# Splitting each weight unit in one piece of 1024 columns instead of two halves of 512

## The chip, the cores and the metric

The kernel runs on one NeuronCore of a Trainium2 chip. The metric is the device time of one execution in microseconds (us). A core has a matmul engine (TensorE, PE in the profile, with PEld for its weight loads), VectorE (DVE), ScalarE (ACT), GpSimd (POOL) and SyncE (SP). Each engine works through its own list of instructions strictly in order; semaphores make an engine wait for another, and DMAs are issued from the lists of SP (queue q1) and ACT (queue q10).

## The reference

A two-layer bidirectional encoder over 512 tokens of width 1024, in float32:

```python
for i in range(DEPTH):                                  # 2 layers
    h = rms_norm(x, norm_mix_g[i])
    q, k, v, u_f, u_s, gates = split(h @ w_in[i])       # 7168 columns
    o = diff_attention(rotary(q), rotary(k), v, lam)    # 8 heads
    y_a = (rms_norm(o, attn_subln_g[i]) * (1 - lam_init)) @ w_attn_br[i]
    y_b = fourier_mix(u_f) @ w_fourier_br[i]
    z = gelu(s5_mix(u_s, ...)) @ w_glu[i] + b_glu[i]    # state-space layer
    y_c = z[..., :D] * sigmoid(z[..., D:])
    g = sigmoid(gates)
    x = x + (g_a * y_a + g_b * y_b + g_c * y_c) @ w_out[i]
    up = rms_norm(x, norm_ffn_g[i]) @ w_up[i]           # 2 x 2816 columns
    x = x + (gelu(conv3(up[..., :D_FF])) * up[..., D_FF:]) @ w_down[i]
    x = x + sigmoid(rms_norm(x, norm_ple_g[i]) @ w_ple_gate[i]) * (p[i] @ w_ple[i])
return rms_norm(x, final_norm_g)
```

## The kernel before

Every large product is done with operands split into a high part that TensorE multiplies fast (float32r) and a low remainder, and three matmuls stand for one: high by high, low by high, high by low (`mm`, L101). Activations are kept transposed: tile `hh`/`hl` number k holds 128 of the 1024 features for all 512 tokens.

Weights come in units of 128 x 1024 float32 (512 KB). A unit is one output tile of 128 columns with all eight k-tiles of 128, so the product of one unit is 24 matmuls of 512 columns into one PSUM bank. `unit` (L85) fetches a unit with one DMA on SP's list into `wr` (two buffers), and then splits it: ACT copies `wr` to the high part `wh`, DVE subtracts that from `wr` to give the low part `wl`. It does so in two halves of 512 columns, each in buffers of its own, six of `wh` and six of `wl`, which all units share. A half holds four k-tiles; its buffer comes free when the last matmul that reads those four k-tiles is done. `unit_wide` (L478) does the same for the V projection with POOL in place of DVE, and `row_unit` (L1056) for the last stage, most of it in 14 buffers of its own pool.

The order of each engine's list is not written out: a scheduler plans it at build time from priorities, data and free buffers, with buffers handed out in the order in which they come free in its plan. It is static on the chip.

A layer runs thus: norm, state-space parameters and Fourier mixing (s5_params, `fourier`); attention by heads (`head`, L520) with the state-space tables (`s5_tables`, L373, POOL) in the background; then the branch products. For what follows one place matters: the turn from attention to the branch products (L821 to L841). There the last head's output `oh`/`ol` number 7 is made; `s5_toeplitz` (L440) and `s5_gather_u` (L608, `U<-usd`, eight DMAs of 16 x 32 x 64 elements) issue many DMAs from ACT's list; and TensorE does the eight products with `w_attn` (L840). A `w_attn` unit multiplies `oh` 0 to 7: its first half needs heads 0 to 3 alone, its second half heads 4 to 7. TensorE starts three of these products early, in three banks `w` of PSUM, and finishes them when the last head is there. After them come eight state-space chunks (`s5_chunk`, L616) mixed with gate and Fourier products, the GLU (L877), `w_out`, the MLP (L919 and L942) and the gated embedding (L970, `ple_last` L988). In the GLU two units at a time (`w2`, then `w1`) serve two output tiles each.

Of the kernel before, what the change touches and what calls it, by code (L numbers as in the profile page):

```python
# [9 lines left out]
F32 = mybir.dt.float32  # L10
F32R = mybir.dt.float32r
I32 = mybir.dt.int32
AF = mybir.ActivationFunctionType
ALU = mybir.AluOpType
# [4 lines left out]
P = 128  # L19
# [31 lines left out]
class Kernel:  # L51
# [33 lines left out]
    def unit(self, src, cols=1024):  # L85
        nc = self.nc
        raw = self.t(self.wp, "wr", (P, 1024), bufs=2)
        nc.sync.dma_start(raw[:, :cols], src)
        out = []
        for c in range(0, cols, 512):  # L90
            n = min(512, cols - c)
            hi = self.t(self.wp, "wh", (P, 512), F32R, bufs=6)
            lo = self.t(self.wp, "wl", (P, 512), F32R, bufs=6)
            nc.scalar.activation(hi[:, :n], raw[:, c:c + n], AF.Copy)  # L94
            nc.vector.tensor_tensor(out=lo[:, :n], in0=raw[:, c:c + n],  # L95
                                    in1=hi[:, :n].bitcast(F32), op=ALU.subtract)
            for i in range(n // P):
                out.append((hi[:, i * P:(i + 1) * P], lo[:, i * P:(i + 1) * P]))
        return out

    def mm(self, ps, w, xh, xl, start=True, stop=True):  # L101
        nc = self.nc
# [171 lines left out]
    def s5_params(self, i, keep, pool, R):  # L274
# [18 lines left out]
        def unit(c, sn):  # L293
# [5 lines left out]
            V.tensor_tensor(out=sn, in0=sn, in1=t, op=ALU.mult)  # L299

        unit(c, sn)
        Wr = self.t(keep, "Wr", (P, 8, n))
        Wi = self.t(keep, "Wi", (P, 8, n))
# [32 lines left out]
        for k in range(3):  # L336
# [3 lines left out]
            V.tensor_tensor(out=c8, in0=t, in1=u, op=ALU.subtract)  # L340
            src = (c8, s8)
        unit(c8, s8)

        ph = []
# [133 lines left out]
    def unit_wide(self, src):  # L478
        nc = self.nc
        raw = self.t(self.wp, "wr", (P, 1024), bufs=2)  # L480
        nc.sync.dma_start(raw, src)
        out = []
        for c in range(0, 1024, 512):
            hi = self.t(self.wp, "wh", (P, 512), F32R, bufs=6)
            lo = self.t(self.wp, "wl", (P, 512), F32R, bufs=6)
            nc.scalar.activation(hi, raw[:, c:c + 512], AF.Copy)
            nc.gpsimd.tensor_tensor(out=lo, in0=raw[:, c:c + 512], in1=hi.bitcast(F32), op=ALU.subtract)
            out += [(hi, lo, 0), (hi, lo, 256)]
        return out

    def qk_proj(self, i, ar, ap, m, tag, hh, hl, cosr, sinr, z=None):
        nc = self.nc
# [563 lines left out]
    def row_unit(self, pool, src, own):  # L1056

        nc = self.nc
        raw = self.t(self.wp, "wr", (P, 1024), bufs=2)
        nc.sync.dma_start(raw, src)  # L1060
        out = []
        for c in range(0, 1024, 512):
            hi = self.t(pool, "lwh", dt=F32R, bufs=14) if own else self.t(self.wp, "wh", dt=F32R, bufs=6)
            lo = self.t(pool, "lwl", dt=F32R, bufs=14) if own else self.t(self.wp, "wl", dt=F32R, bufs=6)
            self.split(raw[:, c:c + 512], hi, lo)
            out.append((hi, lo))
        return out

    def v_pair(self, i, ap, hp, hh, hl, rc):
        nc = self.nc  # L1070
# [149 lines left out]
```

## Time and profile before

| what | value |
|---|---|
| time before, median of 3 runs | 2235.33 us (2235.26 to 2237.52) |
| the profiled execution's own time | 2237.99 us |
| its span in the profile | 2236.2 us |
| TensorE busy | 2121.7 us, 95% |
| VectorE busy | 1534.3 us, 69% |
| ScalarE busy | 1023.5 us, 46% |
| GpSimd busy | 760.2 us, 34% |

The span is what the profile sees from the first to the last instruction; all positions below count from its start. Layer 0 runs to about 1136 us and layer 1 from there on: attention from 110 to 417 and from 1200 to 1517, the turn to the branch products from 417 to 446 and from 1517 to 1546. An instruction's duration is in its row; a number in brackets behind a row is the time that the engine stood idle before it, and what ended that. Matmuls overlap, so the distance from start to start is what one costs on TensorE, not its duration.

### The profile page before, as it was taken

Reading aid. Unit: us, or ns where it says so; the run is one execution under the profiler, and the core shown is the slowest. Engines: PE = TensorE matmul, PEld = TensorE weight load, DVE = VectorE, ACT = ScalarE, POOL = GpSimd, SP = SyncE. Lnnn points to the kernel's source line nnn. Section 1 sums busy time; section 2 is a strip of 40 time slices with the busy share of each in tenths; the row PEclk is TensorE's granted clock in tenths of the full one; section 3 lists DMA queues with packets and bytes.
Section 4 is the critical chain, followed back from the end, with each engine's and each line's share of the span. In section 5 each row is a group of like instructions: output and inputs, shape, how many; then the busy total and the mean of one; then the engine's idle time right before and its main releaser. Section 6 shows DMA issues by size and latency. Waiting matters only on the chain.

```text
span 2236.2 us, 29074 instructions
## 1 busy us (share of the span) xinstructions
PE 2121.7 (95%) x10432; PEld 1772.2 (79%) x10432; DVE 1534.3 (69%) x2664; ACT 1023.5 (46%) x1900; POOL 760.2 (34%) x748
## 2 busy tenths in 40 slices
PE   7888989899999999999998898898999999999998
PEld 5777778688888888888887787687888888888886
DVE  7988997566666766633689899984666667665344
ACT  4256665244434444433442766552445444444333
POOL 4497876223101322200025967841330012221000
PEclk9999999999999999999998999999999999999999
DMA  5232232665323333233432322236743323333341
GB/s 186 79 110 78 86 101 97 190 222 197 116 94 95 97 102 95 92 95 97 149 118 80 105 87 90 97 123 186 259 150 107 97 90 101 97 95 96 95 130 57
DMA packets 117232, 259.20 MB, mean 116 GB/s; under 512 B 43456, under 2 KB 49856, under 8 KB 115040
## 3 DMA queue, kind: packets, MB, share of 16 engines
q1 hardware_dynamic: 87040, 218.48, 31.3%
q10 hardware_dynamic: 30048, 38.87, 5.2%
q8 instruction: 82, 1.34, 0.3%
q14 instruction: 62, 0.51, 0.1%
HBM read 216.87 MB, written 40.37 MB: 115 GB/s over the span
## 4 chain that ended last, share of the span: by engine, by line
PE 69%; DVE 13%; POOL 6%; DMA 5%; ACT 3%; issue 2%; ACTq 0%; SPq 0%; DVEq 0%; POOLq 0%
PE w L106 55%; PE s L106 5%; DVE wl L95 2%; DMA tab<-tb 1%; PE s L639 1%; DVE mx L541 1%; DMA U<-usd 1%; PE w L1079 1%; POOL ra L501 1%; POOL tb L417 1%; DVE tb L402 1%; DVE pr L553 1%; PE w L1026 1%; PE w L1028 1%; PE w L1027 1%
## 5 line engine op out<-in xcount | busy, mean ns | idle before, releaser
L95 DVE TENSOR_TENSOR wl<-wr,wh 128x512 fp32r<-128x512 f32 x596 | 465.5, 785 | 303.5 <-ACT wh L94 295.6
L94 ACT ACTIVATE wh<-wr 128x512 fp32r<-128x512 f32 x596 | 368.5, 624 | 631.4 <-PE w L106 424.7
L106 PE MATMUL w<-hh,wh 128*128 128x512 f32 x1536 | 607.8, 396 | 20.1 <-DVE rs L499 9.0
L106 PE MATMUL w<-hl,wh 128*128 128x512 f32 x1536 | 604.8, 394 | 2.3 <-DVE hl L82 2.2
L106 PE MATMUL w<-hh,wl 128*128 128x512 f32 x1536 | 604.6, 394 | 1.6 <-DVE wl L95 1.6
L106 PEld LDWEIGHTS w<-hh,wh 128*128 128x128 f32 x1536 | 291.6, 190 | 82.5 <-DVE rs L499 10.6
L106 PEld LDWEIGHTS w<-hl,wh 128*128 128x128 f32 x1536 | 291.2, 190 | 63.5 <-DVE hl L82 5.0
L106 PEld LDWEIGHTS w<-hh,wl 128*128 128x128 f32 x1536 | 290.9, 189 | 62.0 <-DVE wl L95 2.2
L180 POOL TENSOR_TENSOR sq<-sq,sq 128x512 f32<-128x512 f32 x18 | 25.0, 1391 | 454.0 <-ACT sq L178 454.0
L191 POOL TENSOR_TENSOR ge<-ge,cv 128x512 f32<-128x512 f32 x44 | 57.8, 1315 | 305.3 <-DVE ge L190 305.3
L106 PE MATMUL w<-ah,wl 128*128 128x512 f32 x352 | 140.4, 399 | 0.0
L106 PE MATMUL w<-al,wh 128*128 128x512 f32 x352 | 138.7, 394 | 0.0
L106 PE MATMUL w<-ah,wh 128*128 128x512 f32 x352 | 138.0, 392 | 0.0
L546 ACT ACTIVATE pr<-s,mx 128x512 f32<-128x512 f32 x128 | 87.9, 689 | 54.5 <-DVE mx L541 49.2
L541 DVE TENSOR_REDUCE mx<-s 128x1 f32<-128x512 f32 x128 | 85.7, 678 | 8.9 <-PE s L540 8.9
L936 POOL TENSOR_TENSOR uu<-uu,cv 128x512 f32<-128x512 f32 x44 | 58.2, 1323 | 71.9 <-DVE cv L193 71.9
L106 PEld LDWEIGHTS w<-al,wh 128*128 128x128 f32 x352 | 66.1, 188 | 17.1
L539 PE MATMUL s<-ks,qs 128*128 128x512 f32 x128 | 56.9, 450 | 23.7 <-ACT pr L546 23.0
L106 PEld LDWEIGHTS w<-ah,wh 128*128 128x128 f32 x352 | 66.1, 188 | 15.8
L106 PEld LDWEIGHTS w<-ah,wl 128*128 128x128 f32 x352 | 66.1, 188 | 15.3
L106 PE MATMUL w<-oh,wh 128*128 128x512 f32 x128 | 52.6, 421 | 14.8 <-DVE m L841 6.5
L553 DVE SCALAR_TENSOR_TENSOR pr<-pr,c,pr 128x512 f32<-128x512 f32 x64 | 65.8, 1028 | 1.0
(417 smaller groups left out, 4227.3 us busy)
## 6 DMA issues: line engine op xcount, KB each, us to landing
wr<-in_w_in SPq DMA_DIRECT2D x112, 512.0 KB
wr<-in_w_up SPq DMA_DIRECT2D x88, 512.0 KB
tb<-tab SPq DMA_DIRECT2D x16, 1536.0 KB
tab<-tb ACTq DMA_DIRECT2D x64, 256.0 KB
wr<-in_w_down SPq DMA_DIRECT2D x32, 512.0 KB
tab<-vbt ACTq DMA_DIRECT2D x32, 256.0 KB
wr<-in_w_attn SPq DMA_DIRECT2D x16, 512.0 KB
wr<-in_w_glu SPq DMA_DIRECT2D x16, 512.0 KB
```

The lines of the kernel that those rows point to most:

```text
L94: nc.scalar.activation(hi[:, :n], raw[:, c:c + n], AF.Copy)
L95: nc.vector.tensor_tensor(out=lo[:, :n], in0=raw[:, c:c + n], in1=hi[:, :n].bitcast(F32), op=ALU.subtract)
L106: nc.tensor.matmul(ps, lhsT=w[i][a], rhs=b[i], start=start and i == 0 and q == 0, stop=stop and i == n - 1 and q == 2)
L180: eng.tensor_tensor(out=sq, in0=sq, in1=acc[c], op=ALU.add)
L191: nc.gpsimd.tensor_tensor(out=sq, in0=sq, in1=y, op=ALU.mult)
L402: nc.vector.tensor_tensor(out=vb, in0=vb, in1=t2, op=ALU.add)
L417: G.tensor_tensor(out=ct, in0=wsel(prm["Wr"], d, d == 1), in1=bsel(2), op=ALU.mult)
L539: nc.tensor.matmul(s, lhsT=q[:, c, qs], rhs=kk[:, c], start=True, stop=False)
L541: V.tensor_reduce(mx[:, c:c + 1], s, op=ALU.max, axis=AX.X, negate=True)
L546: nc.scalar.activation(pt, ss[c], AF.Exp, bias=mx[:, c:c + 1], accum_out=(s1, s2)[c][:, qt:qt + 1])
L553: V.scalar_tensor_tensor(out=pr[0], in0=pr[1], scalar=c2, in1=pr[0], op0=ALU.mult, op1=ALU.add)
L936: G.tensor_tensor(out=u, in0=u, in1=c, op=ALU.mult)
```

## The change

All three helpers split a unit in one instruction per engine, into buffers of 1024 columns, three of `wh` and three of `wl` (seven in the last stage's own pool): the bytes are the same. What reads the parts reads slices of the large buffer. The lists are planned anew by the scheduler.

```diff
@@ unit
-        out = []
-        for c in range(0, cols, 512):
-            n = min(512, cols - c)
-            hi = self.t(self.wp, "wh", (P, 512), F32R, bufs=6)
-            lo = self.t(self.wp, "wl", (P, 512), F32R, bufs=6)
-            nc.scalar.activation(hi[:, :n], raw[:, c:c + n], AF.Copy)
-            nc.vector.tensor_tensor(out=lo[:, :n], in0=raw[:, c:c + n],
-                                    in1=hi[:, :n].bitcast(F32), op=ALU.subtract)
-            for i in range(n // P):
-                out.append((hi[:, i * P:(i + 1) * P], lo[:, i * P:(i + 1) * P]))
-        return out
+        hi = self.t(self.wp, "wh", (P, 1024), F32R, bufs=3)
+        lo = self.t(self.wp, "wl", (P, 1024), F32R, bufs=3)
+        nc.scalar.activation(hi[:, :cols], raw[:, :cols], AF.Copy)
+        nc.vector.tensor_tensor(out=lo[:, :cols], in0=raw[:, :cols], in1=hi[:, :cols].bitcast(F32),
+                                op=ALU.subtract)
+        return [(hi[:, c:c + P], lo[:, c:c + P]) for c in range(0, cols, P)]
@@ unit_wide
-        for c in range(0, 1024, 512):
-            hi = self.t(self.wp, "wh", (P, 512), F32R, bufs=6)
-            lo = self.t(self.wp, "wl", (P, 512), F32R, bufs=6)
-            nc.scalar.activation(hi, raw[:, c:c + 512], AF.Copy)
-            nc.gpsimd.tensor_tensor(out=lo, in0=raw[:, c:c + 512], in1=hi.bitcast(F32), op=ALU.subtract)
-            out += [(hi, lo, 0), (hi, lo, 256)]
-        return out
+        hi = self.t(self.wp, "wh", (P, 1024), F32R, bufs=3)
+        lo = self.t(self.wp, "wl", (P, 1024), F32R, bufs=3)
+        nc.scalar.activation(hi, raw, AF.Copy)
+        nc.gpsimd.tensor_tensor(out=lo, in0=raw, in1=hi.bitcast(F32), op=ALU.subtract)
+        return [(hi, lo, c) for c in range(0, 1024, 256)]
@@ row_unit
-            hi = self.t(pool, "lwh", dt=F32R, bufs=14) if own else self.t(self.wp, "wh", dt=F32R, bufs=6)
-            lo = self.t(pool, "lwl", dt=F32R, bufs=14) if own else self.t(self.wp, "wl", dt=F32R, bufs=6)
-            self.split(raw[:, c:c + 512], hi, lo)
-            out.append((hi, lo))
-        return out
+        hi = self.t(pool, "lwh", (P, 1024), F32R, bufs=7) if own else self.t(self.wp, "wh", (P, 1024), F32R, bufs=3)
+        lo = self.t(pool, "lwl", (P, 1024), F32R, bufs=7) if own else self.t(self.wp, "wl", (P, 1024), F32R, bufs=3)
+        self.split(raw, hi, lo)
+        return [(hi[:, c:c + 512], lo[:, c:c + 512]) for c in (0, 512)]
```

What the new plan does to ACT's list at the turn of layer 0. Before, `wh_5018` and `wh_5022` are the two halves of the fifth `w_attn` unit, `wh_5054` and `wh_5058` those of the sixth; the fourth unit stands further up.

```order
L94 ACTIVATE wh_5018<-wr_5016 128x512
L452 DMA dtab_276<-kfb_1008 128x512
...
L81 ACTIVATE oh_4125<-og_4098,gsub_208 128x512
L78 ACTIVATE ffh_5165<-fraw_5163 128x512
L613 DMA U_4175<-usd_277 16x32x64 x8
L94 ACTIVATE wh_5022<-wr_5016 128x512
L94 ACTIVATE wh_5054<-wr_5052 128x512
L94 ACTIVATE wh_5058<-wr_5052 128x512
```

Now, in the same place, with `wh_4810` for the fourth `w_attn` unit and `wh_4842` for the fifth:

```order
L81 ACTIVATE oh_3997<-og_3970,gsub_204 128x512
L78 ACTIVATE ffh_4973<-fraw_4971 128x512
L605 DMA U_4047<-usd_273 16x32x64 x8
L91 ACTIVATE wh_4810<-wr_4808 128x1024
L91 ACTIVATE wh_4842<-wr_4840 128x1024
```

The split of the whole fourth unit and of the first half of the fifth stood ahead of the eight U DMAs, and stands behind them now. Layer 1 has the same move (`wh_14947` ahead of `U_14104` before; `wh_14091` and `wh_14123` behind `U_13328` now).

TensorE's list at that place, before: `w_4954` is the third `w_attn` product, `w_4990` the fourth (halves `wh_4982` and `wh_4986`), `w_5026` the fifth (halves `wh_5018` and `wh_5022`).

```order
L106 MATMUL w_4954<-oh_4125,wl_4951 128x512
L106 MATMUL w_4990<-oh_1538,wh_4982 128x512
L106 MATMUL w_4990<-ol_1539,wh_4982 128x512
...
L106 MATMUL w_4990<-oh_4125,wl_4987 128x512
L106 MATMUL w_5026<-oh_1538,wh_5018 128x512
...
L106 MATMUL w_5026<-oh_2638,wl_5019 128x512
L106 MATMUL w_5026<-oh_3094,wh_5022 128x512
```

And now: `w_4782` is the third product, `w_4814` the fourth, `w_4846` the fifth.

```order
L101 MATMUL w_4782<-oh_3997,wl_4779 128x512
L101 MATMUL w_4814<-oh_1490,wh_4810 128x512
L101 MATMUL w_4814<-ol_1491,wh_4810 128x512
L101 MATMUL w_4846<-oh_1490,wh_4842 128x512
L101 MATMUL w_4846<-ol_1491,wh_4842 128x512
L101 MATMUL w_4814<-oh_1490,wl_4811 128x512
```

TensorE's sequence of products is the same, but each of the two units is one pair of buffers now, and two matmuls of the fifth product have moved ahead of the fourth's first use of a low part.

## Rows read from the trace of the kernel before

**Rows 1.** The page: busy time, share and instructions of each engine.
```profile
PE 2121.7 (95%) x10432; PEld 1772.2 (79%) x10432; DVE 1534.3 (69%) x2664; ACT 1023.5 (46%) x1900; POOL 760.2 (34%) x748
```

**Rows 2.** Busy time by stretch; columns in the first line.
```profile
core 0: us, PE busy (x) PEld busy (x) DVE busy (x) ACT busy (x) POOL busy (x), PEclk, DMA share, GB/s
...
310.00:360.00 50.00, 44.56 (x216) 36.89 (x215) 45.16 (x77) 33.04 (x71) 35.51 (x33) 0.93 0.26 86
...
417.00:446.00 29.00, 21.57 (x100) 16.62 (x98) 9.56 (x22) 3.79 (x6) 1.36 (x3) 0.94 0.87 231
446.00:612.00 166.00, 165.29 (x883) 141.43 (x884) 106.25 (x143) 78.33 (x130) 42.74 (x35) 1.00 0.58 181
...
1546.00:1720.00 174.00, 174.00 (x914) 148.28 (x915) 110.20 (x150) 80.74 (x134) 42.71 (x35) 0.99 0.55 175
```

**Rows 3.** Chain of waits, MLP of layer 0: start, length, what.
```profile
719.53 353.64 PE w L106 x1543
```

**Rows 4.** Timeline of ACT, turn of layer 0: start, length, engine, line, instruction.
```profile
427.88 0.72 ACT L81 ACTIVATE oh<-og,gsub 128x512 fp32r<-128x512 f32 x1 [3.50 <-DMA dtab<-kfb]
432.97 0.63 ACT L78 ACTIVATE ffh<-fraw 128x512 fp32r<-128x512 f32 x1 [4.38 <-DMA tb<-tab]
432.99 12.99 ACTq L613 DMA_DIRECT2D U<-usd  x8
446.02 1.67 ACT L94 ACTIVATE wh<-wr 128x512 fp32r<-128x512 f32 x3 [12.42 <-DMA U<-usd]
```

**Rows 5.** Timeline of TensorE, same place (36 matmuls from the first to the third row).
```profile
435.04 0.80 PE L106 MATMUL w<-oh,wh 128*128 128x512 f32 x1 [3.94 <-DVE m L841]
...
437.33 0.63 PE L106 MATMUL w<-oh,wl 128*128 128x512 f32 x1
...
444.66 0.40 PE L106 MATMUL w<-oh,wl 128*128 128x512 f32 x1
446.71 0.50 PE L106 MATMUL w<-oh,wh 128*128 128x512 f32 x1 [1.65 <-ACT wh L94]
```

**Rows 6.** Busy time by stretch: those 36 matmuls of layer 0, and layer 1's.
```profile
434.90:446.60 11.70, 10.02 (x36) 7.75 (x36) 1.28 (x3) 0.58 (x2) 0.00 (x0) 0.87 1.20 237
1532.30:1545.90 13.60, 10.22 (x36) 7.82 (x36) 1.25 (x3) 0.63 (x2) 0.00 (x0) 0.87 1.05 225
```

**Rows 7.** Timeline of ACT, turn of layer 1.
```profile
1530.36 14.86 ACTq L613 DMA_DIRECT2D U<-usd  x8
1545.27 1.67 ACT L94 ACTIVATE wh<-wr 128x512 fp32r<-128x512 f32 x3 [14.30 <-DMA U<-usd]
```

**Rows 8.** Timeline of TensorE, turn of layer 1 (36 matmuls to the second row).
```profile
1532.41 0.50 PE L106 MATMUL w<-oh,wh 128*128 128x512 f32 x1 [2.56 <-DVE m L841]
...
1542.24 0.39 PE L106 MATMUL w<-oh,wl 128*128 128x512 f32 x1
1545.95 0.50 PE L106 MATMUL w<-oh,wh 128*128 128x512 f32 x1 [3.33 <-ACT wh L94]
```

**Rows 9.** ACT by line and shape: count, busy, mean ns, idle before.
```profile
L94 ACT ACTIVATE wh<-wr 128x512 fp32r<-128x512 f32 x580 | 361.8, 630 | 618.2 <-PE w L106 420.2 <-issue 54.6 <-PE s L106 35.9
...
L505 ACT ACTIVATE ks<-ra 128x1024 fp32r<-128x1024 f32 x16 | 16.9, 1057 | 11.4 <-POOL ra L501 8.2 <-DVE c L552 3.0
```

**Rows 10.** DVE by line and shape, whole span.
```profile
L95 DVE TENSOR_TENSOR wl<-wr,wh 128x512 fp32r<-128x512 f32 x580 | 458.8, 795 | 303.5 <-ACT wh L94 295.6 <-PE w L106 4.1
...
L95 DVE TENSOR_TENSOR wl<-wr,wh 128x256 fp32r<-128x256 f32 x16 | 6.7, 416 | 0.0
```

**Rows 11.** DVE by line and shape, 720 to 1074, then 110 to 417.
```profile
L95 DVE TENSOR_TENSOR wl<-wr,wh 128x512 fp32r<-128x512 f32 x125 | 89.0, 712 | 99.2 <-ACT wh L94 95.4 <-PE w L106 2.0
...
L95 DVE TENSOR_TENSOR wl<-wr,wh 128x512 fp32r<-128x512 f32 x49 | 49.9, 1024 | 7.1 <-ACT wh L94 7.1
```

**Rows 12.** Chain of waits by line, 110 to 417.
```profile
by line: PE w L106 12.1%; issue 6.9%; DMA tab<-tb 5.4%; POOL ra L501 4.4%; POOL rs L500 3.6%; POOL tb L417 3.5%; DVE wl L95 3.4%; DVE mx L541 3.0%; DVE pr L553 2.8%; DMA tab<-vbt 2.6%; ACT pr L546 2.4%; POOL tb L401 2.4%; POOL tb L240 2.4%;
```

**Rows 13.** Chain of waits, 417 to 447.
```profile
416.55 0.74 POOL tb L243
```

More of the change, by code (lines that the diff above doesn't have):

```diff
@@ L481, in unit_wide @@
         nc.sync.dma_start(raw, src)
-        out = []
-        for c in range(0, 1024, 512):
-            hi = self.t(self.wp, "wh", (P, 512), F32R, bufs=6)
-            lo = self.t(self.wp, "wl", (P, 512), F32R, bufs=6)
-            nc.scalar.activation(hi, raw[:, c:c + 512], AF.Copy)
-            nc.gpsimd.tensor_tensor(out=lo, in0=raw[:, c:c + 512], in1=hi.bitcast(F32), op=ALU.subtract)
-            out += [(hi, lo, 0), (hi, lo, 256)]
-        return out
+        hi = self.t(self.wp, "wh", (P, 1024), F32R, bufs=3)
[3 more added lines that the diff above has]
+        return [(hi, lo, c) for c in range(0, 1024, 256)]
     def qk_proj(self, i, ar, ap, m, tag, hh, hl, cosr, sinr, z=None):
@@ L1060, in row_unit @@
         nc.sync.dma_start(raw, src)
-        out = []
-        for c in range(0, 1024, 512):
-            hi = self.t(pool, "lwh", dt=F32R, bufs=14) if own else self.t(self.wp, "wh", dt=F32R, bufs=6)
-            lo = self.t(pool, "lwl", dt=F32R, bufs=14) if own else self.t(self.wp, "wl", dt=F32R, bufs=6)
-            self.split(raw[:, c:c + 512], hi, lo)
-            out.append((hi, lo))
-        return out
+        hi = self.t(pool, "lwh", (P, 1024), F32R, bufs=7) if own else self.t(self.wp, "wh", (P, 1024), F32R, bufs=3)
+        lo = self.t(pool, "lwl", (P, 1024), F32R, bufs=7) if own else self.t(self.wp, "wl", (P, 1024), F32R, bufs=3)
+        self.split(raw, hi, lo)
+        return [(hi[:, c:c + 512], lo[:, c:c + 512]) for c in (0, 512)]
     def v_pair(self, i, ap, hp, hh, hl, rc):
```

## The prediction

> **What bounds the kernel now.** I read the page's busy shares first, then busy time by stretch, then the chain of waits and the timelines at the places where TensorE stops. TensorE is busy 95% of the span [rows 1], and outside attention practically without a gap: 165.29 of 166 us behind the turn of layer 0, 174.00 of 174 behind that of layer 1 [rows 2]. In the MLP one piece of the chain is 1543 matmuls in 353.64 us, 0.229 us each [rows 3], so a unit of 24 matmuls keeps TensorE for 5.5 us. There, shortening a split gains nothing; what makes TensorE late before such a stretch is paid in full. In attention TensorE and VectorE share the bound (44.56 and 45.16 of 50 us in one slice [rows 2]). And at the turn from attention to the branch products, 29 us with 21.57 busy [rows 2], neither computes what the end waits for: ScalarE's list is held for 12.99 us by the eight U DMAs, and in layer 1 for 14.86 [rows 4, 7].
>
> **The shorter splits.** A DVE split takes 416 ns at 256 columns [rows 10] and 690 to 712 at 512 where nothing disturbs it (712 in the MLP [rows 11]); 256 columns more cost about 0.28 us, so 1024 take about 1.25 us, estimated from these rows, and two halves 1.4: 0.15 us saved per unit. ACT takes 630 ns for 512 and 1057 for 1024 [rows 9]: 0.20 saved. Over some 300 units that is 60 us of ACT and 45 of DVE, but nearly all of it in stretches in which TensorE is the bound. What can count is attention. There a 512 split takes 1024 ns, not 712 [rows 11]: 0.31 us of each is something that the row doesn't explain, presumably GpSimd's work beside it. If that is paid once per instruction, a merged pair saves 0.15 + 0.31 = 0.46 us; if it grows with the columns, 0.15. The middle is 0.31. The 49 splits between 110 and 417 are some 24 pairs: 7.4 us of DVE time a layer. But splits are 3.4% of that stretch's chain [rows 12], 10.4 of their own 49.9 us, a fifth; a fifth of 7.4 is 1.5 a layer, **-3 us** for both. The ends: nothing, or all of 24 x 0.46 x 2 = 22 us if every split were on the chain. Upwards: a DVE instruction of 1.25 us holds what is queued behind it (the softmax maxima, the transposed probabilities) 0.55 us longer than one of 0.7; if each of the 24 stood before such work, 13 us a layer, 26 in all. I take none of this, since the two halves stood in the same list before and only what stood between them is moved.
>
> On the lock between DVE and GpSimd the Trainium skill (SBUF — State Buffer, section "SBUF: two separate sides") says that the loser waits for the whole instruction of the other, when DVE reads two SBUF inputs. The rows' 1024 ns against 712 agree with waits of that kind, but don't tell how many there are. By the rule a pair would save the 0.46 above, and the sum would be 1 us lower.
>
> **Buffers that come free by units.** In the steady stretches two units are ready while a third buffer is refilled: 1.06 us of ACT and 1.25 of DVE, against 5.5 us for each unit in hand. Nothing is lost: TensorE's work hides it, and without that cover it would be 2.3 us a unit. In the GLU two of three buffers are held by the two units in use. The plan hands out the buffer of the unit that ends first, with its pair's last 12 matmuls (2.75 us) still to run; the low part is needed two matmuls later, at 3.2 us, and is there at 2.3 us plus what ACT and DVE have queued ahead. That is tight but fits: zero, with up to 0.9 us for each of three changes of units a layer, 5 us in all, if the queue ahead is longer. At the program's start and in the last stage a whole unit is ready 1 us later than its first half; DMAs and norms cover this: zero, or 2 us.
>
> **The turn.** Here the change costs. Three `w_attn` products wait for the last head with their units in the buffers. Before, the first halves of these units, which need heads 0 to 3 alone, had been read early; their three buffers held the whole fourth unit and the first half of the fifth, split before ACT came to the U DMAs. That is the 36 matmuls that TensorE ran from 435.04 on while ACT was held [rows 5], and 36 again from 1532.41 [rows 8]. Now no buffer is free before the last head has been multiplied. The plan puts both splits behind the U DMAs, and TensorE, whose list has these products next, must wait.
>
> Step by step for layer 0. ACT is free at 446.02 [rows 4]. It splits the fourth unit until 447.08 and the fifth until 448.1; TensorE can begin at 447.14, with the same 0.06 us as before (446.02 + 0.63 to 446.71, rows 4 and 5). It does the two matmuls of each that need a high part alone, and is done with them, and has the first low part (447.1 + 1.25 = 448.4), at about 449.0. Then 44 matmuls remain: 44 x 0.229 = 10.1, to 459.1. Before, at 446.71, 12 of the fifth product remained, to 449.5. Lost: 9.6 us. TensorE stood idle before both runs of 36, and in both its clock was the lower level for a while: granted 0.87 over the stretch [rows 6], and 9.62 us from first to last [rows 5] where 35 x 0.229 is 8.0; in layer 1 9.83 [rows 8]. Before, this 1.6 to 1.8 us lay in time that TensorE waited out anyway; now it is on the path, 0.8 of it already counted with the first four matmuls. So 9.6 + 0.6 to 1.0: about 10.3 a layer. In layer 1 ACT comes free at 1545.27 and TensorE went on at 1545.95 [rows 7, 8], the same distance. Behind each turn TensorE has no gap in which to catch up [rows 2]. **+20.5 us** for both. The ends: nothing, if the U DMAs begin early enough for attention to cover them; 24 us, if the lower clock lasts through more of the products.
>
> **Sum.** -3 + 20.5 = +17.5 on the profiled execution's 2237.99 gives 2255.5. That execution was 2.66 us above the median of the runs, so 2252.8 on the median's scale; I say **2252 us**.
>
> **Rivals.**
> *Attention slows as well.* The longer DVE instructions stand before the maxima and probabilities. For it: DVE is busy nine tenths there. Against: as many columns stood in the list before. Half of the 26 us: 2252 + 13 = 2265.
> *The lock and the fixed costs are the bound.* DVE's saving counts for its most of 22 us, not 3. For it: 1024 against 712 ns. Against: splits are a fifth of their own time on the chain. 2252 - 19 = 2233; with half of it, 2242. By the skill's rule above, as far as it alone goes, 2251; this rival needs the chain to be DVE's as well.
> *The change does nothing at the turn, the kernel is faster.* The chain at the turn begins with the last table on GpSimd, at 416.55 [rows 13], then DMAs, then U. If lighter ACT and DVE lists let the tables end earlier while attention's TensorE work still runs, the U DMAs lie under attention. It decides once they begin some 10 us earlier in each layer: then 20.5 us go, and the 3 stay, 2235.3 - 3 = 2232; the gaps of 1.65 and 3.33 us [rows 5, 8] could go too, 2227. Against: lists that are 7 us a layer shorter, a fifth of that on the chain, are not 10 us earlier.
> *Part of the way.* The U DMAs begin 3 to 5 us earlier in each layer: 2252 - 8 = 2244.
>
> **How the numbers follow.** The forecast, 2246 to 2258 as its own range: 0.60. Part of the way: 0.12. Attention slower: 0.14. DVE's saving in full, about 2233 to 2242: 0.07. No cost at the turn: 0.07. Faster or slower by 0.2% is 4.5 us, about what a measurement of this kernel tells from no change: below 2230.9 or above 2239.8. Faster gets most of the last case and a little of the one before, 0.07. Same gets the rest of the last and much of the one before, 0.07. Slower has 0.86. The range leaves out the last case and part of the neighbours below, and the tail of slower attention: 2239 to 2266.
>
> **What would show it.** In the profile after: no `w_attn` matmuls between the last head's and the end of the U DMAs; a wait of about 16 us of TensorE for the high part at each turn (before: 3.94 + 1.65 and 2.56 + 3.33 with 36 matmuls between); then the fourth product; TensorE still without gaps behind it; about 300 splits of some 1.25 us in the MLP on DVE and 1.06 on ACT. The distance from the end of the U DMAs to the end of layer grows by about 10 us in each layer, and attention (110 to 417) is a few us shorter or equal. I am wrong if the wait at the turn is under 10 us, if attention moves by more than 6 us either way in a layer, or if the GLU shows waits for low parts of more than 1 us each.

## The result: slower by about 1%

The changed kernel takes 2258.69 us (median of 4 runs, 2253.38 to 2260.49), the kernel before 2236.07 beside it (4 runs, 2235.26 to 2237.52): 1.0097 times as long, interval 1.0079 to 1.0114. The forecast was 2252, range 2239 to 2266. The profiled execution took 2260.49 us, its span is 2258.7: 22.5 more than before. What follows is read on the spans of these two profiled executions.

The page of the changed kernel, answering to [rows 1]:

```profile
PE 2123.6 (94%) x10432; PEld 1777.1 (79%) x10432; DVE 1475.2 (65%) x2356; ACT 960.5 (43%) x1576; POOL 762.5 (34%) x732
```

DVE has 59 us less to do and ACT 63 (45 and 60 were worked out ahead), and TensorE practically the same. On balance none of the 122 us came back as time.

The turn of layer 0 in the changed kernel, ACT's timeline (start, length, engine, line, instruction; the bracket is the idle time before it and what ended that), answering to [rows 4]:

```profile
423.65 0.72 ACT L81 ACTIVATE oh<-og,gsub 128x512 fp32r<-128x512 f32 x1 [2.81 <-DMA dtab<-kfb]
427.81 0.63 ACT L78 ACTIVATE ffh<-fraw 128x512 fp32r<-128x512 f32 x1 [3.45 <-DMA tb<-tab]
427.83 13.31 ACTq L605 DMA_DIRECT2D U<-usd  x8
441.19 2.00 ACT L91 ACTIVATE wh<-wr 128x1024 fp32r<-128x1024 f32 x2 [12.74 <-issue]
```

TensorE at the same place, answering to [rows 5]:

```profile
426.48 0.40 PE L101 MATMUL w<-oh,wl 128*128 128x512 f32 x1
442.30 0.80 PE L101 MATMUL w<-oh,wh 128*128 128x512 f32 x1 [15.42 <-ACT wh L91]
442.89 0.63 PE L101 MATMUL w<-ol,wh 128*128 128x512 f32 x1
443.32 0.72 PE L101 MATMUL w<-oh,wh 128*128 128x512 f32 x1
443.84 0.63 PE L101 MATMUL w<-ol,wh 128*128 128x512 f32 x1
444.26 0.63 PE L101 MATMUL w<-oh,wl 128*128 128x512 f32 x1
...
447.25 0.51 PE L101 MATMUL w<-oh,wh 128*128 128x512 f32 x1
447.60 0.39 PE L101 MATMUL w<-ol,wh 128*128 128x512 f32 x1
```

and at the turn of layer 1, answering to [rows 8]:

```profile
1542.66 0.40 PE L101 MATMUL w<-oh,wl 128*128 128x512 f32 x1
1559.11 0.79 PE L101 MATMUL w<-oh,wh 128*128 128x512 f32 x1 [16.04 <-ACT wh L91]
```

ACT's list has the eight U DMAs first and both high-part splits behind them. The third `w_attn` product ends at 426.9, and then TensorE has nothing until 442.30; before, 36 matmuls ran here. After the wait of 15.42 us the distances from start to start are 0.43 us (two of them 0.52 and 0.59) up to 447.25 and 0.23 from 447.60 on. The granted clock of these 5 us (busy time by stretch):

```profile
442.30:447.30 5.00, 5.00 (x12) 3.69 (x13) 2.94 (x3) 1.93 (x3) 0.00 (x0) 0.50 1.14 177
```

0.50, the lower level of 1.2 GHz, behind a wait in which TensorE did nothing.

Where the 22.5 us are is found by cutting the span at the end of the third `w_attn` product and the start of the MLP, in both layers. As the start of the MLP counts DVE's first read of an MLP product (`gp`) in layer 0 and TensorE's next matmul behind that read in layer 1; the differences come out the same by either. These two stretches in the kernel before (columns as in [rows 2]):

```profile
431.10:718.80 287.70, 282.12 (x1390) 236.40 (x1391) 173.73 (x256) 122.99 (x203) 46.96 (x44) 0.99 0.50 152
1529.90:1820.50 290.60, 284.77 (x1392) 237.87 (x1392) 173.80 (x257) 123.27 (x204) 46.92 (x44) 0.99 0.49 151
```

and in the changed kernel:

```profile
426.90:726.40 299.50, 283.53 (x1392) 237.26 (x1392) 166.19 (x213) 115.25 (x159) 48.31 (x44) 0.97 0.49 146
1543.10:1843.00 299.90, 283.40 (x1393) 237.03 (x1393) 165.94 (x214) 116.07 (x160) 48.84 (x44) 0.97 0.49 146
```

The same work, some 1390 matmuls, takes 11.8 us longer in layer 0 and 9.3 in layer 1, together 21.1. Of this, 10.6 and 9.1 are lost by the end of the 48th matmul behind the cut, the work of two products (449.84 before and 456.20 now; 1550.40 and 1572.71). Behind it come 1.4 us more, of which a wait of TensorE for a table (508.50, layer 0) is 0.57; the others were not traced. The rest follows from the ends of these stretches: to the first cut the changed kernel is 4.2 us earlier (431.1 to 426.9); from the MLP of layer 0 to the cut of layer 1 it takes 816.7 us, not 811.1, 5.6 more; from the MLP of layer 1 to the end 415.7 in both. -4.2 + 11.8 + 5.6 + 9.3 = 22.5.

### The profile page after: what moved, and what is told of

The parts are those of the page before. It is cut to its first block, busy times and chain, and to the rows that moved or that the text cites. A ratio compares the mean times of both kernels' runs of the same rounds, so it can differ in the third digit from the quotient of the medians.

```text
span 2258.7 us, 28154 instructions
## 1 busy us (share of the span) xinstructions
PE 2123.6 (94%) x10432; PEld 1777.1 (79%) x10432; DVE 1475.2 (65%) x2356; ACT 960.5 (43%) x1576; POOL 762.5 (34%) x732
## 4 chain that ended last, share of the span: by engine, by line
PE 71%; DVE 15%; POOL 5%; DMA 4%; ACT 2%; issue 2%; ACTq 1%; SPq 0%; DVEq 0%; POOLq 0%
PE w L101 57%; PE s L101 4%; DVE wl L92 2%; DMA tab<-tb 1%; PE s L631 1%; DVE mx L533 1%; DMA tb<-tab 1%; PE o L555 1%; DMA U<-usd 1%; DVE tb L397 1%; POOL tb L412 1%; DVE pr L545 1%; PE m L405 1%; PE w L1068 1%; DVE tb L414 1%
## 5 line engine op out<-in xcount | busy, mean ns | idle before, releaser
L92 DVE TENSOR_TENSOR wl<-wr,wh 128x1024 fp32r<-128x1024 f32 (+1 forms) x298 | 384.7, 1292 | 220.3 <-ACT wh L91 216.8
L91 ACT ACTIVATE wh<-wr 128x1024 fp32r<-128x1024 f32 (+1 forms) x298 | 311.7, 1047 | 460.1 <-PE w L101 317.0
L82 DVE SCALAR_TENSOR_TENSOR al<-uu,ah 128x512 fp32r<-128x512 f32 x44 | 32.6, 741 | 80.9 <-ACT ah L81 80.9
```

The source lines that it names most:

```text
L82: nc.vector.scalar_tensor_tensor(out=lo, in0=src, scalar=scale, in1=hi.bitcast(F32), op0=ALU.mult, op1=ALU.subtract)
L91: nc.scalar.activation(hi[:, :cols], raw[:, :cols], AF.Copy)
L92: nc.vector.tensor_tensor(out=lo[:, :cols], in0=raw[:, :cols], in1=hi[:, :cols].bitcast(F32), op=ALU.subtract)
```

## The experiments

Theory A, the prediction's: the cost is the turn, because both high parts stand behind the U DMAs that hold ACT. Theory B: the long instructions or the wide buffers cost in themselves, at the turn or elsewhere. Theory C, from the second set on: a hold of ACT costs wherever the U DMAs are issued. "Third product to MLP" below is the stretch just shown. Each ratio is against runs of the kernel before on the same chip.

**Big buffers, small instructions** (`e1_big_buffers_small_splits`): the buffers of 1024 columns stay, each filled by two instructions per engine. `unit` is shown; `unit_wide` and `row_unit` are changed alike.

```diff
-        nc.scalar.activation(hi[:, :cols], raw[:, :cols], AF.Copy)
-        nc.vector.tensor_tensor(out=lo[:, :cols], in0=raw[:, :cols], ...)
+        for c in range(0, cols, 512):
+            e = min(c + 512, cols)
+            nc.scalar.activation(hi[:, c:e], raw[:, c:e], AF.Copy)
+            nc.vector.tensor_tensor(out=lo[:, c:e], in0=raw[:, c:e], ...)
```

> Buffers of 1024 columns, three of each, as in the changed kernel, but each unit split by two instructions of 512 columns as before. Theory A (the cost is that a buffer comes free only with its whole unit, so that ACT's splits of the fourth and fifth w_attn units fall behind the U DMAs): the wait of about 15 us for the high part at each turn stays, and the time is 2250 to 2262 us. Theory B (the cost is the longer split instructions, which hold up what is queued behind them in attention): without them the time is back at 2236 to 2241, and the turn has no such wait.

2273.39 us, 1.0167 [1.0147, 1.0187], some 15 us above the changed kernel. TensorE's timeline at the turn of layer 0 in this kernel:

```profile
458.83 0.79 PE L102 MATMUL w<-oh,wh 128*128 128x512 f32 x1 [12.35 <-ACT wh L93]
```

The wait is there without any long instruction, and 13.48 us in layer 1; third product to MLP is 297.8 and 296.3, 10.1 and 5.7 more than before. So the wait comes with the buffers, and B's long instructions are refuted as its cause. But the expected time was missed on the high side: the third product ends at 446.5, 15.4 us later than before. DVE's splits between 110 and 417 don't explain it (44 instructions and 47.4 us, against 49 and 49.9 in [rows 11]); the plan has put other lists together. Why these lists are so much worse stays open.

**U DMAs from SP's list, changed kernel** (`e2_after_u_on_sp`):

```diff
-            nc.scalar.dma_start(U[j * 16:(j + 1) * 16], v[j])
+            nc.sync.dma_start(U[j * 16:(j + 1) * 16], v[j])
```

> The changed kernel with the eight U DMAs issued from SP's list instead of ACT's; ACT's order is otherwise the same. Theory A: ACT splits the fourth w_attn unit right behind the ffh copy, about 12 us earlier at each turn, and TensorE works through two or three units while U lands: 10 us gained per turn, 2236 to 2243 us. If it is DMA traffic or attention that costs (theory B), the time stays at 2253 to 2260. If SP's list is held instead and the weights come late, something between, with TensorE waiting for w_attn units from the third one on.

2250.06 us, 1.0062 [1.0045, 1.0079]; third product to MLP 295.0 and 294.2. ACT's timeline at the turn of layer 0 and TensorE's:

```profile
427.25 0.63 ACT L78 ACTIVATE ffh<-fraw 128x512 fp32r<-128x512 f32 x1 [3.08 <-DMA U<-usd]
427.79 1.99 ACT L91 ACTIVATE wh<-wr 128x1024 fp32r<-128x1024 f32 x2
```

```profile
429.74 0.47 PE L101 MATMUL w<-oh,wh 128*128 128x512 f32 x1 [3.06 <-DVE m L833]
...
431.98 0.79 PE L101 MATMUL w<-oh,wl 128*128 128x512 f32 x1 [0.52 <-DVE wl L92]
...
452.86 0.79 PE L101 MATMUL w<-oh,wl 128*128 128x512 f32 x1 [3.25 <-DVE wl L92]
```

ACT is free, and the wait of 15.42 us for the high part is gone: A's hold is real. But the expected 2236 to 2243 was missed. About half of the cost stays at the turn, 7.3 and 3.6 us against before: the first two splits still come only once the last head is multiplied, and the sixth product waits 3.25 us for its low part, in both layers. The sixth unit's splits:

```profile
447.77 1.04 ACT L91 ACTIVATE wh<-wr 128x1024 fp32r<-128x1024 f32 x1
449.99 1.22 DVE L641 TENSOR_TENSOR_SCAN z<-Rt,z 128x512 f32<-128x512 f32 x1
451.58 1.22 DVE L92 TENSOR_TENSOR wl<-wr,wh 128x1024 fp32r<-128x1024 f32 x1
```

On DVE the low part stands behind work of the first state-space chunk (the scan, `z`). The third case of the expectation, SP's list held and the weights late, is not excluded: the time lies between the other two, as it says, and the sixth unit's fetch was issued at 431.95, behind the U DMAs (420.93 to 427.87) and the tables. What the buffers cost and what SP's list costs was not separated in this kernel.

Busy time and granted clock of this kernel behind the two waits:

```profile
428.00:438.00 10.00, 7.74 (x20) 5.47 (x21) 5.06 (x7) 1.77 (x2) 0.00 (x0) 0.66 1.21 270
452.00:458.00 6.00, 5.14 (x13) 4.03 (x14) 6.00 (x7) 4.33 (x6) 3.03 (x2) 0.52 0.24 87
```

DVE is busy in all 6 us from 452 on, with the low parts among other work; and the clock is down again, 0.66 and 0.52.

**The same in the kernel before** (`e3_before_u_on_sp`):

> The kernel before with the eight U DMAs issued from SP's list. Theory A: only the waits of 1.65 and 3.33 us for the second half of the fifth unit go, 3 to 6 us gained, 2230 to 2233 us; the half buffers had hidden the rest already. Theory B says nothing of it, the same time as before, 2236.

2233.02 us, 0.9996 [0.9982, 1.0009]: no difference that can be measured, some 2 us of median. The 3 to 6 us that A forecast are not shown; by the interval up to 4 are possible. In the trace both waits are gone, and third product to MLP is 288.6 and 284.3, 0.9 more and 6.3 less than before. So the 36 matmuls had covered most of the hold. Its full price it has only together with buffers that come free late.

**Halves freed late in the kernel before** (`e4_before_halves_freed_late`): halves of 512 and their buffers stay; only the order of the eight k-tiles in the `w_attn` products changes, so that the first half stays in use until the last head as well.

```diff
-            self.mm(ps, w, oh, ol)
+            od = (0, 1, 2, 4, 5, 6, 7, 3)
+            self.mm(ps, [w[j] for j in od], [oh[j] for j in od], [ol[j] for j in od])
```

> The kernel before, halves of 512 and all, but each w_attn product takes the heads in the order 0, 1, 2, 4, 5, 6, 7, 3, so that its first half is read until the end and comes free with the second. Theory A: the cost of the turn appears without any change of instruction or buffer size: 8 to 11 us per turn, 2252 to 2259 us, with a wait of 14 to 17 us for the high part at each turn. Theory B: no change, 2236 to 2239.

2250.11 us, 1.0064 [1.0048, 1.008]. TensorE's timeline at the turns of layer 0 and layer 1:

```profile
441.10 0.80 PE L106 MATMUL w<-oh,wh 128*128 128x512 f32 x1 [11.26 <-ACT wh L94]
...
1547.31 0.80 PE L106 MATMUL w<-oh,wh 128*128 128x512 f32 x1 [10.45 <-ACT wh L94]
```

Two thirds of the loss (15.1 of 22.6 us, by the medians) appear with no instruction and no buffer changed in size, and with the same wait. So what costs is when a buffer comes free at this one place. But the sizes were missed, the time by 2 us and the turns by more. By the trace, whose span is 10.6 us above the one before, third product to MLP is 292.8 and 294.2: 5.1 and 3.6 us lost, not 8 to 11 each. The waits are 3 to 4 us below the least expected: at the turn of layer 0 the third product ends at 429.8, 2.3 us after the U DMAs began (427.52), not 0.9 before.

**U gathered early.** In four kernels the U DMAs of a layer are issued ahead of `s5_toeplitz`, into a buffer of their own; the plan issues them 84 us earlier in layer 0 of the changed kernel and 95 in layer 1. The cut diff leaves out that attention's pools are released ahead of this and no longer behind `s5_toeplitz`.

```diff
+        ug = self.pool(f"ug{i}")
+        U = self.s5_gather_u(ug, usd)
         self.s5_toeplitz(i, gp, kfb, dtab)
...
-        U = self.s5_gather_u(s5, usd)
```

Changed kernel, from ACT's list (`e5_after_u_early_act`):

> The changed kernel with the eight U DMAs of each layer issued by ACT some 100 us earlier, in attention, into a buffer of their own, instead of behind the last table. Theory A (the +22 us are the turn: both high-part splits queue behind the U DMAs that hold ACT): the waits of 15.4 and 16.0 us for the high part fall below 5 us, the stretch from the end of the third w_attn product to the first MLP matmul goes from 299.5 and 299.9 back to 287 to 291 each, the time is 2236 to 2243. Theory B (the unit-wide buffers cost at the turn by themselves, since no unit can be split before the last head is done, whoever issues U): waits of 3 to 6 us and a low clock stay, stretch 294 to 296, time 2247 to 2252. Theory C (the hold of ACT only moves into attention, which is then longer): waits at the turn gone, attention 8 to 13 us a layer longer, time 2252 to 2265.

Changed kernel, from SP's (`e6_after_u_early_sp`):

> The same with the U DMAs issued by SP. Theory A and B as for the kernel with ACT; theory C falls away here, since SP holds no splits: by C this kernel is 8 to 20 us faster than the one with ACT, by A and B within 4 us of it.

Kernel before, from ACT's (`e7_before_u_early_act`):

> The kernel before with the U DMAs issued early by ACT. Its 36 matmuls already cover the hold, but 1.65 and 3.33 us of waits for the high part and 3.94 and 2.56 us ahead of them are left. Theory A: the kernel before gains at most these, 0 to 8 us in all, time 2226 to 2235. Theory C: attention longer by 8 to 13 us a layer, time 2250 to 2260. If this kernel is within 3 us of the changed kernel with early U, the unit-wide buffers cost nothing once the hold is gone; if it is 5 us or more faster, part of the cost is theirs alone.

Kernel before, from SP's (`e8_before_u_early_sp`):

> The kernel before with the U DMAs issued early by SP. Theory A: 2226 to 2235, as with ACT. Theory C: faster than the one with ACT by 8 us or more.

| kernel | us | ratio to before | TensorE's longest wait at the turns |
|---|---|---|---|
| changed, early, ACT | 2243.14 | 1.0035 [1.0023, 1.0047] | 1.04, 3.15 (tables) |
| changed, early, SP | 2235.85 | 1.0002 [0.9989, 1.0015] | 1.09, 0.72 (tables) |
| before, early, ACT | 2233.91 | 0.9988 [0.9973, 1.0002] | 0.88 (table), 0.56 |
| before, early, SP | 2232.84 | 0.9982 [0.9971, 0.9992] | under 0.3 |

A's ranges (2236 to 2243 and 2226 to 2235) are met, to within 0.2 us. With U early on SP's list the whole loss of the changed kernel is gone; with U early on ACT's, 7.7 us of it stay. (The stretches of 287 to 291 us that A forecast came out at 282.5 and 287.8 with ACT. They don't compare with those above, since the plan ends the third product at another place, in layer 0 7 us later.) The turn with U early on SP, ACT's timeline:

```profile
421.94 1.04 ACT L91 ACTIVATE wh<-wr 128x1024 fp32r<-128x1024 f32 x1
...
430.16 2.01 ACT L91 ACTIVATE wh<-wr 128x1024 fp32r<-128x1024 f32 x2 [0.76 <-PE w L101]
```

and busy time of the turn:

```profile
410.00:446.00 36.00, 34.91 (x181) 29.18 (x180) 23.54 (x43) 13.49 (x19) 6.13 (x7) 1.00 0.72 239
446.00:612.00 166.00, 166.00 (x872) 141.73 (x871) 91.90 (x109) 68.06 (x97) 41.48 (x32) 1.00 0.54 172
```

Three splits stand where ACT was held, and TensorE is busy in 34.91 of 36 us, at the full clock. B fails here: waits of 3 to 6 us with 2247 to 2252 were its forecast for wide buffers, and TensorE waits for no split at these turns. A caveat: moving U also lets the plan fill this place otherwise, so these kernels show that the loss can go, not that U alone was moved.

Changed and before, both early on SP, are 3.0 us apart, and their intervals overlap: once the turn is open, wide buffers and long instructions cost little or nothing there. Both early on ACT, they are 9.2 apart, with intervals that don't overlap. By the measure that the expectation of `e7` gives (within 3 us nothing, 5 or more a part), a part of the cost with ACT is the wide buffers' own. In neither pair is the changed kernel faster. The eighth kernel is the only one below the kernel before; it gains 0.1 to 0.3% by its interval, about what can be told.

The changed kernel from ACT is 7.3 us slower than from SP. C is right in part: its 8 to 20 between the two was nearly reached, but almost all in layer 1 (MLP, by TensorE's matmul, at 717.24 and 715.65 in layer 0, at 1826.60 and 1816.02 in layer 1). Its 2252 to 2265 with ACT was not. In the kernel before C fails: 1.1 us between the two. Busy time of the changed kernel with U early on ACT, in layer 1:

```profile
1450.00:1500.00 50.00, 45.23 (x225) 37.22 (x224) 40.73 (x73) 25.74 (x60) 24.72 (x28) 0.90 0.54 103
1500.00:1550.00 50.00, 46.85 (x225) 39.50 (x224) 25.51 (x47) 14.73 (x24) 14.26 (x17) 0.93 0.66 220
```

and with U early on SP:

```profile
1450.00:1500.00 50.00, 45.70 (x240) 37.70 (x239) 37.84 (x70) 25.38 (x60) 24.29 (x27) 0.97 0.57 120
1500.00:1550.00 50.00, 49.28 (x255) 41.41 (x254) 32.29 (x54) 18.85 (x28) 17.08 (x19) 1.00 0.64 215
```

TensorE has done 450 matmuls in these 100 us, not 495, with a lower granted clock for part of them and a longer wait for a table (3.15 us against 0.72). Which of the issues started this was not separated.

## Why the prediction was right, and where it was off

**The turn.** Forecast +20.5, measured 21.1 (11.8 and 9.3), of which 19.7 (10.6 and 9.1) lie in the 48 matmuls that were worked out. That the sums agree to 0.6 us is partly luck, since the 1.4 us behind them were not in the sum. It failed in no step that decides: no `w_attn` matmul between the last head's and the end of the U DMAs; a wait of "about 16 us" is 15.42 and 16.04; TensorE begins 1.16 us after ACT's first split can start (441.14 to 442.30), forecast 1.12. The late halves (`e4`) show the mechanism without the change, the early U shows it undone. The first low part is in use 3.12 us after ACT comes free (444.26), forecast 2.98 (446.02 to 449.0). The lower clock was a little dearer: the eleven distances from 442.30 to 447.25 take 4.95 us, 2.4 more than 11 x 0.229, where 1.6 to 1.8 were taken. In layer 1 the loss is smaller than worked out, because the kernel before paid there too. Its TensorE behind the wait of 3.33 us:

```profile
1545.95 0.50 PE L106 MATMUL w<-oh,wh 128*128 128x512 f32 x1 [3.33 <-ACT wh L94]
1546.29 0.40 PE L106 MATMUL w<-ol,wh 128*128 128x512 f32 x1
...
1547.64 0.63 PE L106 MATMUL w<-ol,wh 128*128 128x512 f32 x1
1548.07 0.63 PE L106 MATMUL w<-oh,wl 128*128 128x512 f32 x1
```

From 1547.64 on the distances are 0.43 us; the granted clock from 1545.9 to 1550.9 is 0.66. So the twelve distances from 1545.95 on take 4.25 us, where the working took 2.75 (12 x 0.229) in both layers; in layer 0, behind 1.65 us, they took 2.96, at the full clock (1.00 from 446.7 to 449.7).

**One step was incomplete.** The prediction treats the hold of ACT as what makes the buffers late. With ACT's hold gone, and U where it was, 10.9 of the 21.1 us remain (`e2`): the first two units are still split only behind the last head, a later low part is waited for, and the clock falls behind each wait. How much of this is the buffers' and how much SP's list, held instead, was not separated; with U early on SP, and the same buffers, it is gone (`e6`). The kernel before waits for no low part here.

**The shorter splits.** Forecast -3, measured about +1.4 outside the turns (-4.2 + 5.6), so this term is mis-sized by 4.4 us; with 0.6 at the turn that is the 5.0 between +17.5 and the 22.5 of the spans. The durations were right. DVE's splits in the changed kernel, between 110 and 417 and then between 720 and 1074 (instruction, count, busy us, mean ns, idle time before):

```profile
L92 DVE TENSOR_TENSOR wl<-wr,wh 128x1024 fp32r<-128x1024 f32 x23 | 33.6, 1463 | 6.8 <-ACT wh L91 6.8
```

```profile
L92 DVE TENSOR_TENSOR wl<-wr,wh 128x1024 fp32r<-128x1024 f32 x58 | 73.1, 1261 | 74.0 <-ACT wh L91 74.0
```

1.26 us against the estimate of 1.25. In attention a merged split takes 1463 ns, two halves took 2048: 0.59 saved, more even than the 0.46 that the prediction gave to a stall paid once per instruction. Above the undisturbed time are 0.20 us for a merged split and 0.31 for each half: by these rows the stall goes with the instructions and not with the columns. The Trainium skill (SBUF — State Buffer, section "SBUF: two separate sides") says that of a VectorE instruction with two SBUF inputs and a GpSimd one that reads SBUF the later is blocked for the whole of the earlier. The rows agree with waits of that kind, but no run takes GpSimd's work away, so the lock as their cause is not shown. By that rule alone the sum would have been 1 us lower still, and so further from the result. DVE spends 16.3 us less on splits in this stretch of layer 0 [rows 11], 13.5 of it by merging (23 x 0.59; three halves fall outside the stretch now). Layer 0 reaches the third product 4.2 us earlier, about a third of that. What failed is to take the same gain for layer 1: there the stretch from the last embedding step of layer 0 (1127.0 before, 1136.0 now) to the third product grew from 402.9 to 407.1 us, and the stretch ahead of it, from the MLP of layer 0, from 408.2 to 409.6. The plan gives the two layers different lists, and in `e1` the way to the third product of layer 0 is 15.4 us longer with much the same durations, for a reason that stays open. No run shows which wait in layer 1 took it. So the way to the third product, attention in it, is shorter in layer 0 alone, where the forecast had it shorter or equal in both.

**Buffers that come free by units.** Forecast zero, and next to zero it is: from the MLP of layer 1 to the end 415.7 us in both. In the GLU, for which up to 5 us in all were allowed, the chain has one piece of pure matmuls, as before:

```profile
619.59 35.72 PE s L101 x156
```

35.72 / 156 is 0.229 each; no low part is waited for. TensorE has practically no gap behind the turn (165.43 of the 166 us from 446 to 612; the one wait is that of 0.57 for a table).

**The rivals.** Slower attention in the size of +13 didn't come. DVE's saving in full would have needed 11 us a layer on the chain; 4.2 came in layer 0 and none in layer 1. U did begin earlier in layer 0, at 427.83 instead of 432.99, but the third product ended earlier too, so the wait was no shorter: "part of the way" and no cost at the turn needed U to move against TensorE, not with it. In layer 0 U began 0.9 us behind the end of that product, 1.9 before; in layer 1 0.7 and 0.5.

## What to carry to other kernels

A buffer's size sets when it comes free: before merging two buffers into one, look for the place where a consumer is done with one half long before the other, and what ran meanwhile. Here the chain at that place had the price, and 122 us of engine time saved elsewhere bought nothing. If a burst of DMA issues holds an engine's list, try it at a time when it isn't needed at once, and on a list that nobody waits for (2235.85 from SP's list, 2243.14 from ACT's).

## What the runs showed of the hardware that was not expected

Eight U DMAs of 128 KB held ACT's list in one piece for 13.31 us at the turn (427.83 to 441.14). With the early gather their issues stand between and beside ACT's computing from 344.10 to 349.25, and take 4.7 us in all. Issued from SP's list at the turn, ahead of the tables, they took 6.94 (`e2`). One line's issues in the changed kernel (count, ns of the shortest, median and longest):

```profile
L605 ACTq DMA_DIRECT2D U<-usd x16: 309/509/4424, 427.8 to 1553.5; - x16
```

and in the changed kernel with U early on ACT:

```profile
L605 ACTq DMA_DIRECT2D U<-usd x16: 337/482/1272, 344.1 to 1452.9; - x16
```

The median is nearly the same, the longest is 4.4 us against 1.3. At the turn a table of 1536 KB and two transfers of 256 KB were issued on SP's queue within 1.5 us of the first U DMA; at the early place nothing but the U DMAs was issued between 343 and 352. So the longer hold goes with other transfers under way; which of them makes it, if one does, was not tried.
